# The outputs of the recurrence's chunks: the products with the state of a half of the heads ahead of those with the values, in one bank

## The chip, the core and the metric

The kernel runs on one core of a Trainium2 chip. The metric is the device time of one execution in microseconds (us). The engines of the core run side by side: TensorE (PE in the profile; PEld is its loading of weights), VectorE (DVE), ScalarE (ACT), GpSimd (POOL) and SyncE (SP), which issues the loads of the weights.

## The reference

The program is two transformer blocks in a row over a sequence of 256 tokens, 1024 features wide, the first with 16 meta tokens ahead of it (272 in all) and two layers of its own. Only the mixing of its first layer bears on the change, a linear recurrence over the tokens (16 heads of 64 features):

```python
def step(S, inp):
    r_t, w_t, k_t, v_t, a_t, b_t = inp
    sa = jnp.einsum("bhij,bhj->bhi", S, a_t)
    S = S * w_t[:, :, None, :] + sa[..., None] * b_t[:, :, None, :] + v_t[..., None] * k_t[:, :, None, :]
    y = jnp.einsum("bhij,bhj->bhi", S, r_t)
    return S, y
...
_, ys = lax.scan(step, S0, xs)
```

S is a state of 64 by 64 for each head, decayed at every token (w), with a part removed (a, b) and a key and value added (k, v). The output y of a token is the state read with its receptance r. Around this stand feed-forward blocks, norms, projections, and in the later layers attention.

## The kernel before

The weights stream in from memory in units of 512 KB. Each is split in two parts, and the matmuls of `accum` (L269, through `mm3`, L260 to L263) run three products for each tile of 128 by 128: L261, L262 and L263, which add to the same columns of a bank. These make up most of the program.

The recurrence runs over chunks (`chunks`, L923): chunk 0 is the 16 meta tokens, chunks 1 to 4 have 64 tokens each. Within a chunk, matrix products take the place of the token loop, and from chunk to chunk only the state S goes on. The heads go in pairs, two heads side by side on the 128 partitions: head h of a pair has the partitions OWN[h], 0 to 63 or 64 to 127. A step handles one half q of the heads, four pairs j, eight products (`each`, L939). The steps of a chunk c, with the lines of their matmuls:

- `keys` (L968, ck) and `values` (L982, cv): keys and values by token, on 128 partitions; GpSimd clears a part of the values' buffer UV first (L977);
- `within` (L994, cw): products of the keys with the removal keys and the receptances, masked by VectorE (L996) into a buffer G;
- `of_values` (L1020, co) and `removals` (L1028, cr): what the values and the old state add to the removals; VectorE adds them (L1030);
- `solved` (L1037, cs): the inverse of the chunk applied, copied into UV by VectorE or ScalarE;
- `state` (L1048, ct): the new state, which VectorE finishes (L1051, L1052);
- `out` (L1056, cy): the outputs, below;
- `normal` (L1067, cn): square (L1072), sum by head (matmul, L1074), logarithm and exponential on ScalarE (L1075, L1076), gain and gate on GpSimd and VectorE (L1078 to L1080). In the last two chunks the result is split for the output projection (`split`, L266, L267, into z).

An output has two parts that are added in the bank: the receptances read with the state at the chunk's start (L1063: 64 rows of the array, those of the head, and 64 columns), and the masked products G read with the values of the chunk (L1064: 128 rows, 64 columns). ScalarE or VectorE then copies the bank to the buffer yc (`evac`, L236 to L243). Chunk 0 starts from a zero state and has only the second part.

The order of these steps is a list of names written out by hand (ORDER, L57 to L65); `play` (L406) emits them in that order, and a scheduler may move single instructions past their neighbours. From chunk 1 on it reads: "... cn01 cv2 ct10 cy10 cy11 ck2 cw40 co2 cr21 cr20 cw31 cn10 cs21 cs20 ck3 cn11 ct20 ct21 cv3 cy20 co3 cw41 cr30 cr31 cv4 cy21 cs30 cs31 ct30 ct31 cn21 co4 cn20 ck4 cy30 cr40 cr41 cy31 early cs40 cy40 cn30 cn40 cs41 cy41 cn31 cn41" (the first figure is the chunk, the second the half; `early` splits the outputs of the first chunks). The output projection (`out_proj`, L372) follows; its weights are asked for ahead of time.

The buffers come from rings: `slot` (L425) has seven of one size, which take in turn the masked products G of a chunk, the inputs of the recurrence, and a room that holds the states, removals and outputs of chunk 0 (`room`, L943).

Of the kernel before, what the change touches and what calls it, by code (L numbers as in the profile page):

```python
# [30 lines left out]
OWN = (slice(0, 64), slice(64, 128))  # L31
# [71 lines left out]
class Unit:  # L103
    """Weights to stream in, the products with them, and what follows some units later; held: units before that
    this one's products still read."""
# [6 lines left out]
class Core:  # L112
# [35 lines left out]
    def call(self, fn, ahead=0):  # L148
        """fn between units; before it the parts of as many of those that follow, if they are not there yet."""
        self.items.append((fn, ahead))  # L150
# [16 lines left out]
    def hi(self, u):  # L167
        """Weights in two parts that single-pass products carry exactly: the first."""
        if not u.lo:
            return  # L170
        u.wh = self.wring.tile([128, 1024], F32R, tag="wh", name="wh", bufs=WH)[:u.p, :u.n]
        if u.hi == "A":
            self.A.activation(u.wh, u.wf[:u.p, :u.n], AF.Copy)  # L173
        else:
            self.V.tensor_copy(u.wh, u.wf[:u.p, :u.n])

    def lo(self, u):
        """And the second."""
# [5 lines left out]
    def run(self):  # L184
# [5 lines left out]
        def ahead(i, most=WH):  # L190
            """Loads, first and second parts as far ahead of unit i as their rings reach."""
# [44 lines left out]
    def evac(self, name, out, x, scale=None):  # L236
        """Copies x, by ScalarE or VectorE."""
# [17 lines left out]
    def one(self, pool, name, shape, dt=F32):  # L255
        """A tile that keeps its place as long as the pool."""
# [12 lines left out]
    def accum(self, out, wh, wl, xh, xl, kn, n, k0=0, total=None):  # L269
        """out[m] += sum over k of w[k][m] x[k], weights standing, up to n columns of x moving."""  # L270
# [6 lines left out]
    def rsqrt(self, out, x, scale, eps):  # L277
        """1 / sqrt(x * scale + eps), with a Newton step."""
# [24 lines left out]
    def rms(self, n):  # L303
        """1 / rms by token, on every partition."""
# [5 lines left out]
    def split_tile(self, k, gain, t0, n):  # L310
        """Tile k of h * gain in two parts; its squares added up."""
# [11 lines left out]

    def swiglu(self, win, wout, t0, n, hook, first=()):
        """Reads the split of h that the step before left; hook(k) follows each finished tile of h."""
# [50 lines left out]
    def out_units(self, w, kn, src, scale, t0, n, hook, k0=0, eng=lambda m: {}):  # L376
        """h += scale * x @ w, x split and by features, w given as [m][128][kn][128]; a step a tile of h."""
# [28 lines left out]
    def play(self, order, steps, units):  # L406
        """Emits the steps by name: those of units as they come, the others as calls between them."""
# [7 lines left out]

    def rwkv(self, gain, hook):
# [21 lines left out]
        # the mixed inputs of the projections  # L438
# [6 lines left out]
        def mixes(i, kind, e=None):  # L445
            """Mixed input i, a tile a call: whole, or in two parts."""
# [35 lines left out]
        def first_mix():  # L482
            """The normalised input; the mixed inputs of the keys, the decays and the removals."""
            hn, xx, last = R["hn"], R["xx"], []
            hi, lo = R["x", 2] = [self.xs.tile([128, KT, T], F32R, tag=n, name=n) for n in ("xh", "xl")]
            def mix(x, i, k):
                """Mixed input i, by VectorE, or by ScalarE and GpSimdE."""
# [69 lines left out]
        # keys  # L557
# [18 lines left out]
        def first(n, parts):  # L576
            """The first tiles of the keys and the low-rank pairs of two inputs side by side, as the inputs come."""
# [23 lines left out]
        # low-rank pairs, in float32 products  # L601
        def l1_unit(c0, parts, k0, k1, last, after=()):
            """Columns c0.. of the first factors: parts are (bank, row, width, input)."""
# [67 lines left out]
        # a, b, k by decays within a chunk  # L671
# [5 lines left out]
        def units(q):  # L677
            """1 / norm of the keys."""
# [22 lines left out]
        def over(e, j, x, s):  # L701
            """KB[place j] = x / decay, for the pairs s; the factor -1/2 of place 0 comes with the products."""
# [19 lines left out]
        # strictly lower parts of b a by chunk: diagonal blocks of 32 tokens apart from those beside them  # L722
# [43 lines left out]
        # values, receptance, bonus  # L766
# [24 lines left out]
        # gates  # L791
# [63 lines left out]
    def inverses(self, R):  # L855
        """Inverses of unit lower triangular blocks of 32 tokens (16 in the meta chunk), one per partition."""
# [66 lines left out]
    def chunks(self, R):  # L923
        """The recurrence over chunks of 64 tokens after the 16 of the meta tokens.

        Products that do not need the state of chunk c + 1 fill the waits of chunk c. The values are centred
        by head, and with them all that is linear in them, so that the normalisation needs no mean."""
# [29 lines left out]
        def keys(c):  # L957
            """Keys by token."""
# [15 lines left out]
        def values(c):  # L974
            """Values by token, centred."""
# [10 lines left out]
        def within(c, q, js=(0, 1)):  # L986
            """Products of the chunk's keys with its removal keys and receptances."""
# [11 lines left out]
        def within_meta(r):  # L999
            """The same of the meta chunk, with its removal keys (r = 0) or receptances (1)."""  # L1000
# [13 lines left out]
        def of_values(c):  # L1014
            """What the chunk's values add to the removals."""
# [40 lines left out]
        def out(c, q):  # L1056
            if "yc" not in C[c]:
                C[c]["yc"] = room(2, c)[:, :, :size(c)]
            L, p, UV, g = size(c), self.psum(), C[c]["UV"], C[c]["G"]
            for j, m, h in each(q):  # L1060
                o = p[OWN[h], j * L:(j + 1) * L]
                if c:
                    mm(o, S[c - 1][OWN[h], m], R["AR"][OWN[h], m, 1, tok(c)], start=True, stop=False)  # L1063
                mm(o, UV[:, m, h], g[:, m, h, 1], start=c == 0, stop=True)  # L1064
            self.evac("zy%d" % (2 * c + q), C[c]["yc"][:, qs[q]], p[:, :4 * L].rearrange("p (j t) -> p j t", j=4))

        def normal(c, q):  # L1067
            """Variance by head, gain, bonus and gate."""
# [35 lines left out]
    def doubles(self, R):  # L1104
        """Inverses of 64-token blocks out of those of 32."""
# [99 lines left out]
    def dsa(self, hook):  # L1205
        nc, tc, io = self.nc, self.tc, self.io
        V, A, G, mm = self.V, self.A, self.G, self.mm
        R = {}
# [837 lines left out]
```

## Time and profile before

| | us |
|---|---|
| median of 3 runs | 1602.21 |
| lowest and highest run | 1589.57 and 1602.51 |
| span of the profiled execution | 1588.7 |
| TensorE busy in it | 1527.4 |
| VectorE busy | 1020.3 |
| ScalarE busy | 732.4 |
| GpSimd busy | 334.0 |

The span goes from the first instruction to the last; a run's time is taken around it. The profiled execution's own time is not listed, so the three runs stand beside its span. In the trace each float32 product of the recurrence is two instructions of TensorE (the count behind an x). A tile form like 64*64 or 128*64 is the part of the array that an instruction uses, rows by columns. The granted clock is in parts of the full 2.4 GHz: 1.0, or 0.5 for the lower level of 1.2 GHz; between them lies a mean over a stretch with both.

### The profile page before, as it was taken

To read this page: it belongs to the slowest core of one execution; us is meant where nothing else is said; L and a number is where in the kernel's file an instruction comes from. 1 tells how busy PE (TensorE), PEld (TensorE's weight loads), DVE (VectorE), ACT (ScalarE), POOL (GpSimd) and SP (SyncE) were. 2 spreads that over 40 slices of the span, in tenths; PEclk is the share of its full clock that TensorE was granted. 3 is DMA by queue.
4 is the path that set the end of the run, shared out by engine and by line. 5 is a ranking of instruction groups with operands and counts; after the bars stand their busy time and mean duration, and the time that the engine had idled before them with its cause. 6 is when DMAs were issued, how large, how long until landed. Compare 5 with 4: busy or idle time off the path is not lost.

```text
span 1588.7 us, 30959 instructions
## 1 busy us (share of the span) xinstructions
PE 1527.4 (96%) x12612; PEld 1427.2 (90%) x12612; DVE 1020.3 (64%) x1857; ACT 732.4 (46%) x1266; POOL 334.0 (21%) x346
## 2 busy tenths in 40 slices
PE   7999989699999999999999999899999999999999
PEld 7999967568788999999999987579999978899999
DVE  6655478997444655556555569667665489886643
ACT  6544428333223544445444434655445335566532
POOL 2111034752011111001111043142110334320000
PEclk9999989798888999999999999999999999999999
DMA  7645534121101445555545552036556552265552
GB/s 224 216 173 166 178 96 141 63 92 69 41 1 41 173 173 175 171 175 191 175 174 165 172 166 77 21 112 234 186 183 180 175 167 91 85 215 186 187 195 101
DMA packets 70851, 230.63 MB, mean 145 GB/s; under 512 B 7827, under 2 KB 12468, under 8 KB 70580
## 3 DMA queue, kind: packets, MB, share of 16 engines
q1 hardware_dynamic: 68480, 225.35, 42.7%
q10 hardware_dynamic: 2228, 3.29, 0.9%
q8 instruction: 99, 1.62, 0.4%
q14 instruction: 44, 0.36, 0.1%
HBM read 226.52 MB, written 2.10 MB: 144 GB/s over the span
## 4 chain that ended last, share of the span: by engine, by line
PE 82%; DVE 12%; ACT 2%; DMA 2%; issue 1%; POOL 1%; SPq 0%; DVEq 0%; POOLq 0%; ACTq 0%
PE mm L261 22%; PE mm L262 22%; PE mm L263 22%; DVE wl L182 1%; PE mm L1064 1%; PE mm L1892 1%; PE mm L1063 1%; PE mm L1166 1%; PE mm L1165 1%; PE mm L1167 1%; DVE tf L871 1%; DMA wf<-ffn_in 1%; PE mm L994 1%; DVE u L868 1%; PE mm L1869 1%
## 5 line engine op out<-in xcount | busy, mean ns | idle before, releaser
L173 ACT ACTIVATE wh<-wf 128x1024 fp32r<-128x1024 f32 (+2 forms) x404 | 411.8, 1020 | 538.3 <-issue 284.3
L261 PE MATMUL mm<-xh,wh 128*128 128x272 f32 (+2 forms) x1888 | 544.4, 290 | 14.7 <-ACT wh L173 9.0
L182 DVE TENSOR_TENSOR wl<-wf,wh 128x1024 fp32r<-128x1024 f32 (+2 forms) x388 | 463.1, 1194 | 140.7 <-PE mm L263 96.5
L262 PE MATMUL mm<-xl,wh 128*128 128x272 f32 (+2 forms) x1888 | 542.0, 288 | 3.1 <-DVE xl L440 2.7
L263 PE MATMUL mm<-xh,wl 128*128 128x272 f32 (+2 forms) x1888 | 542.4, 288 | 1.7 <-DVE wl L182 1.7
L261 PEld LDWEIGHTS mm<-xh,wh 128*128 128x128 f32 (+1 forms) x1888 | 356.8, 190 | 21.9 <-ACT wh L173 9.9
L262 PEld LDWEIGHTS mm<-xl,wh 128*128 128x128 f32 (+1 forms) x1888 | 357.2, 189 | 7.5 <-DVE xl L440 3.8
L263 PEld LDWEIGHTS mm<-xh,wl 128*128 128x128 f32 (+1 forms) x1888 | 357.5, 190 | 3.2 <-DVE wl L182 2.7
L261 PE MATMUL mm<-hh,wh 128*128 128x272 f32 (+1 forms) x704 | 201.9, 287 | 0.0
L263 PE MATMUL mm<-hh,wl 128*128 128x272 f32 (+1 forms) x704 | 201.7, 287 | 0.0
L262 PE MATMUL mm<-hl,wh 128*128 128x272 f32 (+1 forms) x704 | 201.7, 287 | 0.0
L352 POOL TENSOR_TENSOR s<-s,rstd 128x272 f32<-128x272 f32 (+1 forms) x88 | 74.6, 849 | 442.8 <-ACT s L351 442.8
L182 POOL TENSOR_TENSOR wl<-wf,wh 128x1024 fp32r<-128x1024 f32 (+3 forms) x58 | 121.3, 2093 | 146.5 <-PE mm L263 63.5
L261 PEld LDWEIGHTS mm<-hh,wh 128*128 128x128 f32 x704 | 132.6, 188 | 0.0
L263 PEld LDWEIGHTS mm<-hh,wl 128*128 128x128 f32 x704 | 132.5, 188 | 0.0
L262 PEld LDWEIGHTS mm<-hl,wh 128*128 128x128 f32 x704 | 132.5, 188 | 0.0
L360 DVE TENSOR_TENSOR u<-mm,s 128x272 f32<-128x272 f32 (+1 forms) x88 | 38.5, 437 | 123.8 <-PE mm L263 108.2
L298 POOL TENSOR_TENSOR acc<-acc,sq 128x272 f32<-128x272 f32 (+1 forms) x48 | 41.4, 863 | 262.9 <-ACT sq L296 247.1
L350 DVE TENSOR_TENSOR t<-mm,rstd 128x272 f32<-128x272 f32 (+1 forms) x88 | 38.2, 436 | 69.8 <-PE mm L263 69.7
L261 PE MATMUL mm<-hid,wh 128*128 128x256 f32 x256 | 72.0, 281 | 0.0
L262 PE MATMUL mm<-hid,wh 128*128 128x256 f32 x256 | 72.0, 281 | 0.0
L263 PE MATMUL mm<-hid,wl 128*128 128x256 f32 x256 | 72.0, 281 | 0.0
(482 smaller groups left out, 2320.4 us busy)
## 6 DMA issues: line engine op xcount, KB each, us to landing
wf<-ffn_in SPq DMA_DIRECT2D x176, 512.0 KB, 3.6
wf<-ffn_out SPq DMA_DIRECT2D x64, 512.0 KB, 3.5
wf<-b_ff SPq DMA_DIRECT2D x64, 512.0 KB, 4.7
wf<-ffn_out SPq DMA_DIRECT2D x32, 384.0 KB, 3.1
wf<-rk_k SPq DMA_DIRECT2D x8, 512.0 KB, 3.4
wf<-rk_v SPq DMA_DIRECT2D x8, 512.0 KB, 3.8
wf<-rk_r SPq DMA_DIRECT2D x8, 512.0 KB, 3.2
wf<-rk_o SPq DMA_DIRECT2D x8, 512.0 KB, 3.2
```

The lines of the kernel that those rows point to most:

```text
L173: self.A.activation(u.wh, u.wf[:u.p, :u.n], AF.Copy)
L182: (self.V if u.lo == "V" else self.G).tensor_tensor(u.wl, u.wf[:u.p, :u.n], u.wh.bitcast(F32), op=ALU.subtract)
L261: self.mm(out, wh, xh, start=start, stop=False)
L262: self.mm(out, wh, xl, start=False, stop=False)
L263: self.mm(out, wl, xh, start=False, stop=stop)
L298: self.G.tensor_tensor(self.acc[:, :n], self.acc[:, :n], self.sq[:, :n], op=ALU.add)
L350: V.tensor_tensor(t[:, :n], st.pop(("g", m))[:, :n], r, op=ALU.mult)
L352: G.tensor_tensor(s[:, :n], s[:, :n], r, op=ALU.mult)
L360: V.tensor_tensor(u[:, :n], st.pop(("u", m))[:, :n], st.pop(("s", m))[:, :n], op=ALU.mult)
L868: e.tensor_tensor(tmp[:, x - o:y - o, :w], a[:, s, x:y, None].to_broadcast([P, y - x, w]), t[:, s:w, :w].to_broadcast([P, y - x, w]), op=A ...
L871: e.tensor_tensor(t[:, x:y, :w], t[:, x:y, :w], tmp[:, x - o:y - o, :w], op=ALU.add)
L994: mm(ps[h][:, j * w:(j + 1) * w], flat(src(c, m)[OWN[h]]), R["AR"][OWN[h], m, j0:j0 + n, tok(c)], start=True, stop=True)
```

## The change

`out` writes the eight products with the state first, then the eight with the values. Before, the two products of a head stood one behind the other. Each head's columns are still added up in the bank. The flag `start`, which marks the first product that goes to an area of a bank, was set for every product with the state; now it is set for the first one in each half of the partitions (j = 0), and the two products of a head are no longer neighbours, for which a check of the builder is turned off.

```diff
             L, p, UV, g = size(c), self.psum(), C[c]["UV"], C[c]["G"]
+            o = lambda j, h: p[OWN[h], j * L:(j + 1) * L]
+            if c:
+                for j, m, h in each(q):
+                    mm(o(j, h), S[c - 1][OWN[h], m], R["AR"][OWN[h], m, 1, tok(c)], start=j == 0, stop=False,
+                       skip_group_check=True)
             for j, m, h in each(q):
-                o = p[OWN[h], j * L:(j + 1) * L]
-                if c:
-                    mm(o, S[c - 1][OWN[h], m], R["AR"][OWN[h], m, 1, tok(c)], start=True, stop=False)
-                mm(o, UV[:, m, h], g[:, m, h, 1], start=c == 0, stop=True)
+                mm(o(j, h), UV[:, m, h], g[:, m, h, 1], start=c == 0, stop=True, skip_group_check=c > 0)
```

The lines behind it move down by four: L1063 becomes L1065, L1064 becomes L1068, L1074 becomes L1078, L1079 becomes L1083. The rest of the diff takes out comments.

TensorE's order in chunk 2, from the new state and the values of the next chunk (L1048, L982) to the first step of the outputs, before; mm is a bank, AR holds the receptances, room the state, UV the values:

```order
L1048 MATMUL mm_4998<-UV_4808,KBt_3913 64x64
L1048 MATMUL mm_5009<-UV_4808,KBt_3913 64x64 x8
L982 MATMUL mm_5022<-mats_81,vf_3054 64x128 x4
L1048 MATMUL mm_4998<-UV_4808,KBt_3913 64x64 x7
L982 MATMUL mm_5028<-mats_81,vf_3054 64x128 x4
L1063 MATMUL mm_5034<-AR_2503,room_4593 64x64
L1064 MATMUL mm_5034<-G_4715,UV_4808 64x64
```

And now:

```order
L1048 MATMUL mm_4998<-UV_4808,KBt_3913 64x64
L1048 MATMUL mm_5009<-UV_4808,KBt_3913 64x64 x8
L982 MATMUL mm_5022<-mats_81,vf_3054 64x128 x4
L1048 MATMUL mm_4998<-UV_4808,KBt_3913 64x64 x7
L982 MATMUL mm_5028<-mats_81,vf_3054 64x128 x4
L1065 MATMUL mm_5034<-AR_2503,room_4593 64x64 x8
L1068 MATMUL mm_5034<-G_4715,UV_4808 64x64 x8
L1020 MATMUL mm_5052<-UV_5020,G_4638 64x64 x16
```

Before, the last two rows are followed by seven more such pairs; now the eight products with the state are one row, and the eight with the values another, with L1020 (co3) right behind them as before.

TensorE's order behind the second step of chunk 1 (mm_4851), before; G_4715 are the masked products of chunk 2:

```order
L1063 MATMUL mm_4851<-AR_2503,room_3954 64x64
L1064 MATMUL mm_4851<-G_4336,UV_4352 64x64
L968 MATMUL mm_4869<-mats_81,kbx_2510 128x128 x4
L968 MATMUL mm_4875<-mats_81,kbx_2510 128x128 x4
L994 MATMUL mm_4882<-AR_2503,kbx_2510 128x128 x4
L994 MATMUL mm_4883<-AR_2503,kbx_2510 128x128 x4
L1020 MATMUL mm_4894<-UV_4808,G_4715 64x64
L1028 MATMUL mm_4912<-room_4593,AR_2503 64x64 x8
L1028 MATMUL mm_4922<-room_4593,AR_2503 64x64 x3
L1020 MATMUL mm_4894<-UV_4808,G_4715 64x64 x15
L1028 MATMUL mm_4922<-room_4593,AR_2503 64x64 x5
```

And now:

```order
L1065 MATMUL mm_4851<-AR_2503,room_3954 64x64 x8
L1068 MATMUL mm_4851<-G_4336,UV_4352 64x64 x8
L968 MATMUL mm_4869<-mats_81,kbx_2510 128x128 x4
L968 MATMUL mm_4875<-mats_81,kbx_2510 128x128 x4
L994 MATMUL mm_4882<-AR_2503,kbx_2510 128x128 x4
L994 MATMUL mm_4883<-AR_2503,kbx_2510 128x128 x4
L1020 MATMUL mm_4894<-UV_4808,G_4715 64x64
L1028 MATMUL mm_4912<-room_4593,AR_2503 64x64 x7
L1020 MATMUL mm_4894<-UV_4808,G_4715 64x64 x15
L1028 MATMUL mm_4912<-room_4593,AR_2503 64x64
L1028 MATMUL mm_4922<-room_4593,AR_2503 64x64 x8
```

The keys (L968) and masked products (L994) stand behind the step as they did; the removals of the first half (L1028) go around L1020 a little differently, four products of them behind it that stood ahead.

## Rows read from the trace of the kernel before

**Rows 1.** The page: its first line, and TensorE in its first part
```profile
span 1588.7 us, 30959 instructions
...
PE 1527.4 (96%) x12612; PEld 1427.2 (90%) x12612; DVE 1020.3 (64%) x1857; ACT 732.4 (46%) x1266; POOL 334.0 (21%) x346
```

**Rows 2.** Stretches: us, busy of PE, PEld, DVE, ACT, POOL (instructions), clock, DMA share, GB/s
```profile
425.83:437.04 11.21, 11.21 (x67) 8.01 (x65) 1.19 (x4) 1.06 (x3) 0.68 (x1) 0.63 0.01 1
437.04:445.85 8.81, 8.81 (x81) 7.90 (x82) 3.90 (x7) 1.57 (x4) 1.63 (x2) 0.50 0.00 0
...
453.40:457.51 4.11, 4.11 (x39) 3.10 (x40) 1.35 (x4) 0.59 (x1) 0.00 (x0) 1.00 0.00 0
...
462.50:466.75 4.25, 4.25 (x33) 3.13 (x32) 0.00 (x0) 0.00 (x0) 0.00 (x0) 0.95 0.00 0
...
473.54:477.65 4.11, 4.11 (x33) 3.03 (x33) 1.02 (x3) 1.64 (x4) 1.40 (x1) 1.00 0.02 4
...
478.63:482.69 4.06, 4.06 (x38) 2.98 (x35) 1.21 (x3) 0.39 (x2) 0.95 (x1) 1.00 0.00 0
484.04:487.90 3.86, 3.86 (x31) 2.84 (x30) 0.85 (x2) 0.89 (x2) 0.00 (x0) 1.00 0.00 0
...
490.03:497.55 7.52, 7.48 (x40) 4.93 (x36) 2.60 (x7) 1.68 (x6) 0.41 (x1) 0.51 0.01 2
497.55:503.90 6.35, 5.47 (x22) 5.29 (x23) 2.04 (x5) 2.41 (x6) 0.00 (x0) 0.50 0.00 0
```

**Rows 3.** The chain that ended last, 400 to 505 us: start, us, what
```profile
421.93 0.60 PE mm L1064 x16
...
429.44 0.40 PE mm L1064 x2
...
443.90 1.90 PE mm L1020 x30
...
453.47 0.25 PE mm L1063 x2
453.72 0.26 PE mm L1064 x2
...
457.58 0.93 PE mm L1020 x31
...
459.60 1.08 PE mm L1028 x32
...
477.72 1.08 PE mm L1028 x32
...
482.76 0.61 PE mm L1037 x16
```

**Rows 4.** The timeline of the output projection: start, us, engine, line, operation
```profile
502.18 0.43 PE L261 MATMUL mm<-z,wh 128*128 128x272 f32 x1
...
502.40 0.43 PE L262 MATMUL mm<-z,wh 128*128 128x272 f32 x1
...
502.63 0.43 PE L263 MATMUL mm<-z,wl 128*128 128x272 f32 x1
```

**Rows 5.** The timeline of VectorE behind the second step of chunk 1
```profile
436.74 2.48 DVE L996 TENSOR_TENSOR G<-mm,tri 128x512 f32<-128x512 f32 x4 [9.91 <-PE mm L1063]
```

**Rows 6.** The timeline behind the second step of chunk 2
```profile
466.75 1.97 PE L1037 MATMUL mm<-room,Tt 64*64 64x64 f32 x32
466.86 0.59 ACT L239 ACTIVATE UV<-mm 64x512 f32<-64x512 f32 x1 [7.72 <-PE mm L1064]
...
468.20 0.36 ACT L239 ACTIVATE UV<-mm 64x256 f32<-64x256 f32 x1
...
468.66 0.59 PE L1048 MATMUL mm<-UV,KBt 128*64 128x64 f32 x6
```

**Rows 7.** The timeline behind the last step
```profile
498.43 1.22 PE L1074 MATMUL mm<-sqc,mats 128*128 128x256 f32 x2 [0.92 <-ACT sqc L1072]
...
502.02 0.43 DVE L267 TENSOR_TENSOR z<-bb,z 128x256 fp32r<-128x256 f32 x1 [0.48 <-ACT z L266]
```

## The prediction

> **What bounds the kernel now.** I read the page's first part, then the stretches of the recurrence, then the chain of waits inside them. TensorE is busy for 96% of a span of 1588.7 us [rows 1], so a saving on it counts wherever it has no idle time. The changed step is called eight times with the state, twice (for the two halves of the heads) in each of chunks 1 to 4, all between 425.8 and 497.6 us. In its stretches TensorE is busy for the whole length, while VectorE and ScalarE are busy for 1.2 of the first 11.2 us and for nothing at all of 462.50 to 466.75 [rows 2]. So here TensorE alone sets the pace, and it does so with tiny matmuls: a step is 8 products with the state and 8 with the values, and each of them is two instructions in the trace.
>
> What one costs stands in the chain: a product with the state holds it for 0.25 us, the next with the values for 0.26, at full clock [rows 3], at 453.47 and 453.72; 16 make the 4.11 us of 453.40 to 457.51 [rows 2]. At the lower clock one holds it for 0.40, at 429.44 [rows 3]. The same shapes cost a quarter of that where they stand with their own kind. L1028 is the twin of the state half (weights and outputs 64 by 64, the halves of the array in turn): 32 instructions in 1.08 us, 0.034 each, at 459.60 [rows 3]. L1020 is the twin of the values half (128 rows, 64 columns, 64 moving): 31 in 0.93, 0.030 each. The values half of the meta chunk, which has no state, stands alone already: 16 instructions in 0.60, though with 16 columns moving [rows 3]. So of 0.257 us per product some 0.19 is neither streaming nor loading; it comes with the change from a product of one kind to one of the other.
>
> Two explanations fit that far. One is the change of the part of the array in use, from 64 rows to 128 and back, at which the array empties. The other is that the second product adds to the columns that the first has just written. The rows are against the second: L261, L262 and L263 add to the same columns one right after the other, and start 0.22 us apart at the lower clock [rows 4], which is 272 columns at 1.2 GHz (0.227) and leaves nothing for a wait.
>
> The Trainium skill has the first as a rule (TensorEngine Tiling (Array Packing), Key Properties): changing the tiling mode, not just the tile, drains TensorE. The trace agrees, by the 0.257 us beside 0.034 and 0.030.
>
> **The change part by part.** It removes and adds no instruction: 16 products a step before and after, the same operands, one evacuation. It turns 16 changes of kind a step into 2. On VectorE and ScalarE one instruction each changes places with its neighbour, on TensorE besides four products of L1028 are on the other side of L1020, and on GpSimd and SP the order is what it was, so only TensorE's own time and what it uncovers count.
>
> The new price of a step: the state half like L1037 x16 directly behind a product with the values, 0.61 us at 482.76 [rows 3], which has one change in it; the values half like 16 of L1020, 0.48, with one change, about 0.6. I take 1.2. From below it is 32 instructions at 0.03, 1.0; from above each change keeps its full 0.19 on top of the streaming, 1.4. Between them lie only 1.5 us over eight steps.
>
> Step by step, at the profiled execution's own times [rows 2]:
> - Steps of chunk 1: 11.21 us become 2.4. Gain 8.8. The granted clock averages 0.63 there: it is 1.0 for about 2.9 us and then 0.5, which is 1.2 GHz. The price of 1.2 a step assumes that it doesn't fall.
> - The stretch behind it, 437.04 to 445.85, is all at 0.5. It came back at the end of a dense block of L1020 (30 in 1.90 us, twice the price at full clock [rows 3]). The fall came inside a row of products that mostly wait; the dense blocks of small products ahead of that row had left the clock at 1.0. I take it that dense halves keep it up: 8.81 becomes 4.4. Gain 4.4; if it falls all the same, nothing here, and 2 less in the line above.
> - What is late next there: VectorE waits 9.9 us for a matmul of L1063 [rows 5], because the products of chunk 2 (G, L996) go into the buffer that holds the first state, whose last reader is the second step of chunk 1. That wait ends with the state half, so L996's 2.5 us move forward with the rest and end near the time at which L1020 wants them. I book nothing.
> - Chunk 2: 4.11 and 4.25 become 2.4. Gain 6.0. Behind the second step stands ScalarE's queue, which that step keeps from starting: from L1037's start at 466.75 four ScalarE items end at 468.56, and only then L1048 goes [rows 6]. L1037 itself took that long, as the clock was low. At full clock it would take 1.1 and TensorE would wait for the rest, so the 1.9 us stay; no gain and no loss.
> - Chunk 3: 4.11 and 4.06 become 2.4. Gain 5.8.
> - Chunk 4, first half: 3.86 and one product that stands ahead of a variance product (0.25) become 1.2. Here the cover goes: ScalarE's logarithm and exponential for the step before ran under the products and now stand ahead of the evacuation. I book 0.4 for it. Gain 2.5.
> - Chunk 4, second half, with a variance product in it: 490.03 to 497.55, 7.52, mostly at 0.5. It becomes 0.6 for the state half, 0.6 for the variance product (half of the 1.22 that one takes at the lower clock [rows 7]) and 0.6 for the values half, 1.8. Gain 5.7.
> - The tail: from the evacuation to the last part of z is VectorE's and ScalarE's, and the output projection's second half needs it [rows 7]. Half of L1074's 1.22 would come back at full clock; I book 0.5.
>
> Sum: 8.8 + 4.4 + 6.0 + 5.8 + 2.5 + 5.7 + 0.5 = 33.7 us, 2.1% of the span. Behind it the feed-forward blocks are TensorE's alone, with weights loaded ahead while the DMA engines lie idle here, so the gain goes through to the end. The span would be 1588.7 - 33.7 = 1555.0. What lies around it isn't shown: the three runs are 1589.57, 1602.21 and 1602.51, so it is 0.9 us if the profiled execution was like the lowest, 13.5 if it was like the median. From the median I get 1602.2 - 33.7 = 1568.5, and forecast 1569. That these runs differ by 13 us with the same program is the widest single term of my range.
>
> **Rivals.**
> 1. The halves gain, but the clock falls as before, by its own timing. Then the stretch behind chunk 1 gives nothing (-4.4), chunk 1's steps 2 less, the last block about 2 less: gain 25, 1577. For it: the clock also fell near 466 and 490 with TensorE busy throughout. Against it: each fall lies in or behind a row of alternating products.
> 2. Only the state half gets cheaper. Its neighbours use different halves of the rows, those of the values half all use 128, so a load of weights might not run beside a product there. Then the 8 products with the values keep 0.257 each, a step costs 2.06 + 0.61 = 2.7, and the gain is 1.4 in each of five steps, about 6 in chunk 1 and 2 at the end: 15, 1587. Against it: L1020's 0.030 an instruction [rows 3].
> The Trainium skill states what would do this (TensorE: Matmul & The Clock Gate, Part 3, What overlaps and what doesn't): weight loads overlap running matmuls only when the row groups differ. The trace disagrees for this shape, by the 0.93 us for 31 of L1020.
> 3. Slower: uncovered waits on VectorE and ScalarE leave TensorE with holes from chunk 1 on, and the clock goes to 0.5 and stays there. From 437.04 to 497.55 some 33 us are not these steps (60.5 less 4.11, 4.25, 4.11, 4.06, 3.86 and 7.52); 12 of them are at 0.5 already (8.8, and about 3 behind 466.75, where L1037 runs at half speed [rows 6]), so 21 more are added; the steps at twice 1.2 still give back about 20. It is then even, and each microsecond of work of the projection and the blocks behind that stays at 0.5 adds one: after 16 us of them it is 1% slower, with the whole projection and the first tiles behind it (26) 1628. For it: the gain in cover is real, and after the last fall half speed lasted to 503.9 [rows 2]. Against it: it needs the clock to stay low through dense work, and dense work brought it back each time.
> 4. No change by over 1%: the recurrence's own chain (removals, inverse, state, through VectorE and ScalarE) sets the pace, so that what TensorE gives up turns into waits. From L1028 at 459.60 to the next at 477.72 is 18.1 us [rows 3]; with both steps cut it is 12.2, while the chain in it is about 2 for the removals and 7 from L1037 at 466.75 to the next step at 473.54 [rows 2, 6]. It would have to grow by 3 us in each chunk to eat a third of the gain; to get below 16 us of gain takes more. I give it little.
>
> **How the numbers follow.** The drain goes and the clock holds, 0.56: 1569. Rival 1, 0.25: 1577. Rival 2, 0.09: 1587. Rival 4, 0.07: 1590. Rival 3, 0.03. A measurement of this kernel tells about 1% from no change, 16 us: faster is below 1586.2, slower above 1618.2. The first two cases and a third of rival 2 are faster, 0.84; with some of rival 4 I say 0.86; same 0.11, slower 0.03. The range goes from the gain in full with a median like the lowest run of before (1589.6 - 33.7 = 1556) to rival 2 (1587).
>
> **What would show it right or wrong.** Right: in the chain of the changed kernel each step appears as a piece of 16 for the state (L1065) and one of 16 for the values (L1068), 0.5 to 0.65 us each, and no piece of two at 0.25; VectorE's 9.9 us behind the state half shrinks; the granted clock is 1.0 from chunk 1 to the next chunk. Rival 1 shows as 0.5 in that stretch. Rival 2 shows as pieces of L1068 of 2 us. Rival 4 shows as idle time of TensorE with VectorE or ScalarE as its releaser. The forecast is wrong if L1068's instructions still stand 0.1 us apart or more, or if new idle time on TensorE between 425 and 500 us is over 10 us.

## The result, and the profile after

| | before | after |
|---|---|---|
| median of 4 runs each, us | 1595.89 | 1553.22 |
| lowest and highest run | 1588.59 and 1602.51 | 1552.98 and 1554.51 |
| span of the profiled execution | 1588.7 | 1551.4 |
| its own time | not listed | 1553.19 |
| mean granted clock in it | 0.971 | 0.984 |

The first of these medians stands beside the 1602.21 of three runs from which the forecast started; one run has been added. The changed kernel takes 0.973 of the time of before, interval 0.970 to 0.977. The forecast was 1569 us with a range of 1556 to 1587: the direction is right, and the time is 2.8 us below the range. The two medians lie 42.7 us apart and the two spans 37.3; the difference is that the profiled execution of before was at the low end of its kernel's runs.

The page of the changed kernel, its first line and TensorE in its first part, against [rows 1]:

```profile
span 1551.4 us, 30960 instructions
...
PE 1489.5 (96%) x12612; PEld 1398.2 (90%) x12612; DVE 1018.1 (66%) x1857; ACT 731.8 (47%) x1266; POOL 334.7 (22%) x346
```

The instructions of the engines are the same in number. The span is 37.3 us shorter, TensorE's busy time 37.9, and the other engines' is where it was within 2.2: what went was TensorE's own time.

The stretches of the changed kernel that answer to [rows 2]: the two steps of chunk 1, the stretch from there to chunk 2, the two steps of chunk 2, the two of chunk 3, the first 9.5 us of the output projection, and the recurrence as a whole (columns as in [rows 2]):

```profile
425.06:427.51 2.45, 2.45 (x65) 2.18 (x66) 1.46 (x4) 0.98 (x3) 0.27 (x1) 1.00 0.03 7
427.51:439.97 12.46, 12.46 (x199) 10.88 (x200) 9.66 (x21) 4.74 (x10) 1.98 (x3) 1.00 0.01 1
439.97:441.20 1.23, 1.23 (x39) 1.16 (x40) 1.20 (x4) 0.59 (x1) 0.00 (x0) 1.00 0.00 0
446.19:447.44 1.25, 1.25 (x35) 1.11 (x36) 0.00 (x0) 0.00 (x0) 0.00 (x0) 1.00 0.00 0
453.58:454.81 1.23, 1.23 (x35) 1.10 (x36) 0.69 (x3) 1.23 (x4) 0.00 (x0) 1.00 0.00 0
455.89:456.97 1.08, 1.08 (x34) 0.95 (x32) 0.95 (x2) 0.41 (x2) 1.08 (x2) 1.00 0.00 0
...
465.51:475.00 9.49, 9.49 (x77) 9.49 (x77) 4.60 (x8) 4.33 (x8) 0.00 (x0) 1.00 0.01 4
...
425.00:500.00 75.00, 72.10 (x1001) 66.72 (x1001) 50.70 (x95) 38.95 (x79) 13.40 (x16) 1.00 0.20 68
```

A step takes 1.08 to 1.25 us in place of 3.9 to 5.6 (7.5 with a variance product in it), and the column of the clock is 1.00 in every row, where five of the rows of the same work before had 0.50 to 0.95. TensorE idles for 2.9 of the 75 us.

The chain that ended last in the changed kernel, against [rows 3] (start, us, what): the steps of chunk 1; the second step of chunk 2 and what follows it; the first half of chunk 4 behind its products with the state.

```profile
425.06 0.61 PE mm L1065 x16
425.67 0.62 PE mm L1068 x16
426.29 0.61 PE mm L1065 x16
426.90 0.62 PE mm L1068 x16
...
446.80 0.64 PE mm L1068 x16
...
447.46 0.59 ACT UV L239
...
448.81 0.37 ACT UV L239
...
...
458.04 0.64 PE mm L1078 x2
...
458.71 0.48 ACT sqc L1079
...
459.21 0.42 ACT sqc L1080
459.63 0.28 ACT room L239
```

Pieces of two at 0.25 us have become pieces of sixteen at 0.61. Behind chunk 2's second step the chain now goes through four ScalarE items, from 447.44 to 449.22, where L1037 at half clock covered them before [rows 6]. TensorE itself works for most of that time; its timeline there, with its idle time in brackets:

```profile
447.35 1.15 PE L1037 MATMUL mm<-room,Tt 64*64 64x64 f32 x32
448.67 0.33 PE L1048 MATMUL mm<-UV,KBt 128*64 128x64 f32 x2 [0.17 <-DVE UV L243]
449.22 0.57 PE L1048 MATMUL mm<-UV,KBt 128*64 128x64 f32 x12 [0.23 <-ACT UV L239]
```

So it idles for 0.40 us there. In chunk 4 ScalarE's logarithm and exponential (L1079, L1080) stand ahead of the copy of the outputs.

VectorE's wait for the first state's last reader, against [rows 5] (who waits for whom: us in total, times, longest):

```profile
DVE G L996 <- PE mm L1065: 1.0, 1, 1.0
```

It was 9.9 us.

Put side by side by TensorE's own sequence (its pieces are the same products in nearly the same order), the changed kernel is 0.8 us ahead at the first of the steps, 34.2 us at the projection's first piece (465.51 in place of 499.66), 36.1 some 20 us into the projection, and 37.3 at the end. So the recurrence and the projection's start give 35.3; the remaining 2.0 are no work of the change: 0.8 lie ahead of it, 1.2 behind it, where the largest piece, 1.8, is a short fall of the clock near 1360 us that of these two executions only the one of before has. The profiles of experiments 7 and 9 have a fall at the same place of the program, so it needs no products in turn.

### The profile page after: what moved, and what is told of

It is laid out like the page before. It is cut to its first block, busy times and chain, and to the rows that moved or that the text cites. A ratio compares the mean times of both kernels' runs of the same rounds, so it can differ in the third digit from the quotient of the medians.

```text
span 1551.4 us, 30960 instructions
## 1 busy us (share of the span) xinstructions
PE 1489.5 (96%) x12612; PEld 1398.2 (90%) x12612; DVE 1018.1 (66%) x1857; ACT 731.8 (47%) x1266; POOL 334.7 (22%) x346
## 4 chain that ended last, share of the span: by engine, by line
PE 82%; DVE 12%; ACT 2%; DMA 1%; issue 1%; POOL 1%; SPq 0%; DVEq 0%; POOLq 0%; ACTq 0%
PE mm L261 23%; PE mm L262 23%; PE mm L263 23%; DVE wl L182 1%; PE mm L1896 1%; PE mm L1170 1%; PE mm L1169 1%; PE mm L1171 1%; DMA wf<-ffn_in 1%; DVE tf L871 1%; PE mm L1873 1%; PE mm L994 1%; PE mm L1898 1%; PE mm L1840 1%; PE mm L982 1%
```

## The experiments

The theory at this point: a change of the number of rows in use (64 and 128) costs some 0.15 to 0.2 us, the drained rows of products pull the granted clock down, both are gone, the sum of the prediction holds, and the base from which it was taken off does not. Five of the experiments test the mechanism and its places (2 to 6), three whether more is to be had (7, 9, 10), and four the base and the spread (1, 8, 11, 12). In the diffs below `o(j, h)` are the columns of a head in the bank.

**1. The kernel before again, unchanged.** What lies around the span, and what spreads?

> The kernel before, unchanged, to see what its two levels of time are (two runs near 1589, two near 1602). Theory A (the alternating products let the clock fall, and how much of the recurrence lies at 1.2 GHz differs from run to run): the runs near 1602 have a span about 12 us longer and a lower mean granted clock, by about 0.008, than those near 1589, whose clock is 0.971. Theory B (the 12 us lie around the span, in the launch): all runs have a span near 1589 and a clock of 0.971.

Measured: 1596.18 us (1588.94 to 1602.48, 12 runs) beside 1594.08 of 17 runs of the same kernel, ratio 1.0006 (0.9987 to 1.0025). The time is 1.74 to 1.93 us above the span in every run, whether it is long or short. The spans go from 1587.1 at a mean clock of 0.974 to 1600.6 at 0.965, with runs at all values between, so it is a spread and not two levels. In the mean clock that is 0.009 of 1594 us, which at 0.5 in place of 1.0 are 29 us, half of them lost where TensorE sets the pace: 14, and the spans differ by 13.5. The mean clock doesn't explain all of it: the spans at 0.965 alone go from 1594.8 to 1600.6. So the profiled execution of before was a run of some 1590.5 us, and the median from which the forecast started lies at the upper end, where the runs of this group have a mean clock of 0.965 or 0.966.

**2. In turn as before, but in two banks**, so that no product adds to what its neighbour has just written. The products with the state are left out of the output; a copy of one of their columns by VectorE stands for their use.

```diff
+            p2 = self.psum() if c else None
             for j, m, h in each(q):
                 if c:
-                    mm(o, S[c - 1][OWN[h], m], R["AR"][OWN[h], m, 1, tok(c)], start=True, stop=False)
-                mm(o, UV[:, m, h], g[:, m, h, 1], start=c == 0, stop=True)
+                    mm(p2[OWN[h], j * L:(j + 1) * L], S[c - 1][OWN[h], m], R["AR"][OWN[h], m, 1, tok(c)], start=True, stop=True)
+                mm(o(j, h), UV[:, m, h], g[:, m, h, 1], start=True, stop=True)
```

> The two kinds of products stand in turn as before, but into two banks, so that none adds to columns just written; the state's part is left out of the outputs, and VectorE reads a column of its bank. Theory A (the change between 64 and 128 rows of the array empties it): a product in turn still holds TensorE for 0.25 to 0.26 us at full clock, 4.1 us a step where the order is in turn. Rival B (adding to columns that the product before has just written waits for it): 0.03 us an instruction, about 1.1 us a step.

Measured: 1582.56 us, one run, span 1580.8. The scheduler happened to pull the products of chunk 1's steps apart into pieces of sixteen and ten, so its time tells little; its pieces tell more. The chain of this kernel, in the first step of chunk 1 and in the next chunk, where the products still stand in turn:

```profile
427.44 0.61 PE mm L1064 x16
428.05 0.61 PE mm L1065 x16
...
443.64 0.26 PE mm L1064 x2
443.90 0.26 PE mm L1065 x2
444.16 0.25 PE mm L1064 x2
```

In turn they take 0.25 and 0.26 as before, in two banks as in one, and grouped 0.61. Adding in the same bank is not the price.

**3. In turn and in one bank as before, but the product with the state on all 128 rows**, like the one with the values. It then adds the other head's rows too, so the outputs are other numbers.

```diff
-                    mm(o, S[c - 1][OWN[h], m], R["AR"][OWN[h], m, 1, tok(c)], start=True, stop=False)
+                    mm(o(j, h), S[c - 1][:, m], R["AR"][:, m, 1, tok(c)], start=True, stop=False)
```

> The two kinds in turn as before and in one bank, but the product with the state takes all 128 rows (both heads of the pair, so the outputs are not the reference's): the same part of the array as the product with the values. Theory A (emptying at a change between 64 and 128 rows): no change is left, 0.03 to 0.06 us a product, 1.0 to 1.2 us a step, and a total near 1553. Rival B (adding to columns just written): 0.25 us a product, 4.1 us a step, total near 1589.

Measured: 1553.51 us, one run, span 1551.7, clock 0.984, the time of the changed kernel. The timeline of TensorE in chunk 1's steps:

```profile
425.89 0.34 PE L1063 MATMUL mm<-AR,room 128*64 128x64 f32 x4
426.01 0.34 PE L1064 MATMUL mm<-G,UV 128*64 128x64 f32 x4
426.13 0.34 PE L1063 MATMUL mm<-AR,room 128*64 128x64 f32 x4
```

The two kinds still alternate, four instructions every 0.12 us, and nothing waits: 0.03 an instruction. Two kinds of operands, two destinations and two lines cost nothing; with 64 rows against 128 the same alternation cost 0.257 a product. So it is the change of the rows, shown by this run beside the second one. It is the rule of the Trainium skill that changing the tiling mode drains TensorE (TensorEngine Tiling (Array Packing), Key Properties), and the trace agrees, with 0.03 against 0.13 an instruction. That the products with the values, all on 128 rows, stand 0.03 apart with their weight loads is against one sentence of the Trainium skill's other page (TensorE: Matmul & The Clock Gate, Part 3, What overlaps and what doesn't), by which loads run beside products only where the row groups differ. The paragraph ahead of that sentence, though, names loads into a background weight buffer as a second case; which of the two holds here no run shows.

**4. Half as many changes as before**: both heads of a pair with the state, then both with the values; 8 changes a step, where before had 16 and the changed kernel has 2.

```diff
+            for j, m in four(q):
+                if c:
+                    for h in range(2):
+                        mm(o(j, h), S[c - 1][OWN[h], m], R["AR"][OWN[h], m, 1, tok(c)], start=True, stop=False, skip_group_check=True)
+                for h in range(2):
+                    mm(o(j, h), UV[:, m, h], g[:, m, h, 1], start=c == 0, stop=True, skip_group_check=c > 0)
```

> Two products with the state, then the two with the values, pair by pair: 8 changes of kind a step, between 16 (before) and 2 (after). If the cost is per change: 4.11 and 1.22 us a step give 0.206 us a change, so 2.45 us a step at full clock. If it is per neighbour in the same columns (Rival B): each product with the values has one other product in between, so something between 1.2 and 2. The clock: if a row of mostly waiting products brings it down, less of the recurrence is at 0.5 than before; total 1563 to 1575.

Measured: 1561.81 us (1559.58 to 1564.3, 4 runs), ratio 0.979 (0.976 to 0.981), 1.2 us below the range expected. The stretch of the recurrence (columns as in [rows 2]), with the clock at 1.00:

```profile
425.00:475.00 50.00, 47.64 (x778) 38.94 (x773) 27.08 (x63) 22.09 (x52) 9.96 (x12) 1.00 0.01 4
```

The chain in chunk 2's first step:

```profile
444.98 0.26 PE mm L1064 x4
445.24 0.27 PE mm L1067 x4
445.51 0.26 PE mm L1064 x4
```

A block of four instructions (two heads) takes 0.26, which is what a block of two took in turn; the step takes 2.11 us (444.98 to 447.09), less than the 2.45 expected. Through blocks of 4 (0.265) and of 16 (0.615) goes a line of 0.029 an instruction and 0.147 a change; the block of 2 lies 0.05 above it. So the price of a change was mis-sized in the prediction: 0.15 between blocks of more than one product, not 0.19. Why a second head in a block adds nothing is not shown: the products of a pair with the state use different halves of the rows, but those with the values both use all rows and cost the same. Over the recurrence this kernel gains 28.7 us, 6.6 less than the changed one; eight steps of 2.11 in place of about 1.22 make 7.1.

**5. and 6. The change in chunk 1 only, and in chunks 2 to 4 only.** Each is the changed kernel with a condition on the chunk, `grouped = c == 1` in the one and `grouped = c != 1` in the other; where it is false the products stand in turn:

```diff
+            grouped = c == 1
+            if c and grouped:
+                for j, m, h in each(q):
+                    mm(o(j, h), S[c - 1][OWN[h], m], R["AR"][OWN[h], m, 1, tok(c)], start=j == 0, stop=False, skip_group_check=True)
             for j, m, h in each(q):
+                if c and not grouped:
+                    mm(o(j, h), S[c - 1][OWN[h], m], R["AR"][OWN[h], m, 1, tok(c)], start=True, stop=False)
```

> Grouped in chunk 1 alone, in turn in chunks 2 to 4. Theory A (each change of kind costs its time, and rows of products in turn let the clock fall): the two steps of chunk 1 take 1.22 us each, the clock stays at 1.0 up to chunk 2, and the gain up to the end of chunk 1's successors is 13 to 16 us; six steps stay at 4.1 or more, so the median is 1575 to 1583, and the runs still spread over 5 us or more, by what the clock does in chunks 2 to 4. Rival C (the clock falls by its own timing, whatever the order of the products): the clock falls in or behind chunk 1 all the same, and the gain there is 7 to 9.

> Grouped in chunks 2 to 4, in turn in chunk 1. Theory A: the clock falls in chunk 1's steps or behind them as before and costs up to 6 us there; six steps at 1.22 us give 18 us, and with the clock at 1.0 at the end 20 to 24: median 1568 to 1576, a spread of a few us. Rival C: falls to 0.5 in chunks 3 and 4 as before, median 1574 to 1582.

Measured: 1578.8 us (1575.42 to 1586.41, 4 runs), ratio 0.990 (0.987 to 0.993), with chunk 1 alone; 1566.79 (1565.08 to 1571.17, 4 runs), ratio 0.983 (0.980 to 0.987), with chunks 2 to 4. The stretches of the recurrence with chunk 1 alone grouped:

```profile
425.00:450.00 25.00, 25.00 (x408) 21.58 (x405) 14.58 (x32) 7.94 (x17) 2.26 (x3) 1.00 0.01 2
450.00:475.00 25.00, 24.59 (x284) 18.68 (x283) 8.24 (x19) 8.17 (x19) 4.62 (x5) 0.96 0.00 1
475.00:505.00 30.00, 28.18 (x193) 25.40 (x194) 15.73 (x28) 14.78 (x30) 4.02 (x6) 0.81 0.21 70
```

And with chunks 2 to 4 grouped:

```profile
425.00:450.00 25.00, 25.00 (x230) 20.22 (x230) 9.14 (x19) 5.61 (x12) 2.31 (x3) 0.66 0.00 1
450.00:475.00 25.00, 23.49 (x489) 20.14 (x488) 15.20 (x35) 12.17 (x29) 6.50 (x7) 1.00 0.01 3
475.00:505.00 30.00, 28.61 (x235) 28.42 (x232) 20.99 (x33) 17.62 (x33) 4.64 (x6) 1.00 0.40 130
```

Where the products are grouped the clock stays at 1.00; where they stand in turn it falls, in these rows of products or behind them (0.96 and 0.81 in the later stretches of the one kernel, 0.66 in the first of the other). By TensorE's sequence the first gives 13.6 us and the second 22.5, together 36.1 beside 35.3 for both at once: the parts add up, and the fall is of their own making, not the program's timing.

**7. The products with the state earlier.** As a step of their own (`out_state`, named cx in the order), ahead of the products with the values: directly behind the removals or solved values, which use 64 rows as well, so that one more change goes and TensorE has work while it waits.

```diff
-          "cs11 cn00 gate7 cw20 cy01 ct11 cn01 cv2 ct10 cy10 cy11 ck2 cw40 co2 cr21 cr20 cw31 cn10 cs21 cs20 "
+          "cs11 cx10 cx11 cn00 gate7 cw20 cy01 ct11 cn01 cv2 ct10 cy10 cy11 ck2 cw40 co2 cr21 cr20 cw31 cn10 "
+          "cs21 cs20 cx20 cx21 ck3 cn11 ct20 ct21 cv3 cy20 co3 cw41 cr30 cr31 cv4 cy21 cs30 cs31 cx30 cx31 ct30 "
+          "ct31 cn21 co4 cn20 ck4 cy30 cr40 cr41 cx40 cx41 cy31 early cs40 cy40 cn30 cn40 cs41 cy41 cn31 cn41 ").split()
...
+        def out_state(c, q):
+            L, p = size(c), self.psum()
+            C[c]["yp", q] = p
+            for j, m, h in each(q):
+                mm(p[OWN[h], j * L:(j + 1) * L], S[c - 1][OWN[h], m], R["AR"][OWN[h], m, 1, tok(c)], start=j == 0, stop=False,
+                   skip_group_check=True)
```

> The state half of the outputs is a step of its own, behind the inverse's products (L1037), or in chunk 4 behind the removals (L1028), which use the same 64 by 64 part of the array; the values half stays where it is, mostly beside products on 128 rows. Theory A: the two changes of a step are nearly gone, 0.15 us each, 2 to 2.5 us in all, and the state halves fill TensorE's wait for ScalarE behind L1037 in chunk 2 (another 0.8): median 1549 to 1552. Rival D (what is saved on TensorE turns into waits on VectorE's and ScalarE's chain): 1553, no change against the changed kernel.

Measured: 1552.76 us (1551.84 to 1554.75, 4 runs), ratio 0.974 (0.971 to 0.976); the changed kernel beside it (below) 1553.97. Theory A's range is missed by 0.8, and the 1.2 us to the changed kernel are less than either kernel's runs differ by. By TensorE's sequence it is 2.8 us ahead of the changed kernel's first profile up to chunk 4, 1.8 at the projection's first piece, and 0.9 at the end. The chain in chunk 4:

```profile
454.05 1.51 DVE z L267
455.56 0.34 DVE room L1030
...
456.04 0.68 PE mm L1037 x16
```

VectorE's subtraction of the early split stands ahead of its addition of the removals, and L1037 waits for that; TensorE idles for 0.98 us. So the earlier products are a gain of 2.8 us, of which chunk 4 takes 1.0 back. Most of the rest of the lead goes in a fall of the clock between 1305 and 1325 us (0.91 there, 1.00 in the changed kernel), which is not the change's.

**8. The changed kernel again**, beside it.

> The changed kernel once more beside the others, for its spread and as the reference of e7: median 1553, a span 1.8 us below each run's time, all runs within 3 us, a clock of 0.984 in each.

Measured: 1553.97 us (1553.5 to 1557.05, 4 runs), ratio 0.975 (0.972 to 0.977); the runs lie 3.6 us apart, a little more than expected.

**9. The seventh kernel with both halves of that subtraction on GpSimd; 10. the same with another order at the end of chunk 4; 11. the changed kernel a third time.**

```diff
-                self.split(z[:, 0, qs[q], :e], z[:, 1, qs[q], :e], R["bb"][q][:, :, :e], (V, G)[q])
+                self.split(z[:, 0, qs[q], :e], z[:, 1, qs[q], :e], R["bb"][q][:, :, :e], G)
...
-          "ct31 cn21 co4 cn20 ck4 cy30 cr40 cr41 cx40 cx41 cy31 early cs40 cy40 cn30 cn40 cs41 cy41 cn31 cn41 ").split()
+          "ct31 cn21 co4 cn20 ck4 cy30 cr40 cr41 cx40 cx41 cy31 cs40 cs41 early cy40 cn30 cy41 cn40 cn31 cn41 ").split()
```

> The kernel e7_placed (the state halves as steps of their own, right behind the removals and the solved values), with both halves of the subtraction in the early split of z on GpSimd instead of one on VectorE. In e7_placed VectorE's subtraction (1.51 us, behind ScalarE's first part) stood ahead of its addition of the removals, L1030, and chunk 4's L1037 went only at 456.0. Theory: that subtraction is the whole of what chunk 4 lost; without it L1037 of chunk 4 goes 2 us or more earlier and the lead of e7_placed behind chunk 3, some 2 to 3 us over the changed kernel, stays to the end: median 1549 to 1551.5, and 1.5 to 3 us below the changed kernel beside it. Rival: ScalarE's own queue of chunk 4 (squares, logarithms, exponentials, copies) ends last there, and takes it back: 1552 to 1554, within 1 us of the changed kernel. Second rival: the split's second half comes later from GpSimd (its work is slower), and the projection waits for it: above 1554.

> The same as e9_gpsimd_split, with the end of the order written by hand changed too: the solved values of both halves of chunk 4 first, then the early split, then the outputs and their normalisation. Theory: ScalarE's parts of the early split no longer stand ahead of the copies that the solved values and outputs need, so 1 us or so more than e9_gpsimd_split: 1548 to 1551. Rival: the split then ends late and the first products of the projection wait for z, so nothing or a loss against e9_gpsimd_split: 1552 to 1555.

> The changed kernel once more, beside the two others on the same chip: 1552.5 to 1555.5, all runs within 4 us of each other, as before, with the time 1.7 to 2.0 us above the span in each run. If the narrow spread of the changed kernel had been chance, a run at 1560 or above would show.

Measured, six runs each: 1552.64 us (1552.2 to 1557.34), 1554.53 (1553.34 to 1557.8) and 1557.76 (1553.55 to 1560.19); ratios 0.973, 0.974 and 0.976, each within 0.004. The chain of the ninth kernel in chunk 4 has no VectorE or GpSimd ahead of L1037:

```profile
455.02 0.62 PE mm L1069 x16
455.63 0.61 PE mm L1037 x16
```

But the first of them goes at 455.63, 0.4 us earlier, or 1.0 with the later start of this execution's recurrence (0.6) taken off, and not 2 or more: TensorE's own products now fill the time up to there, and the 0.98 us that it had idled was all there was to get. With it the loss of chunk 4 is gone, as the theory had it; the size was wrong. It stays 2.9 us ahead of the changed kernel's profiled execution from the recurrence on, until a fall of the clock between 1315 and 1335 us (0.91 there, 1.00 in the changed kernel) takes 1.9 of it; in time it is 0.6 to 5.1 us below the three groups of the changed kernel, and these differ by 4.5 among themselves. So its median is the lowest of all, by an amount that these runs don't tell from nothing. The tenth has 1.3 less of a lead behind the recurrence than the ninth: its rival holds.

The third group of the changed kernel had a run at 1560.19, and its median is 2.3 us above the range expected, so the narrow spread of its first two groups was in part chance. Its profiled execution is 4.5 us behind the first one already at 315 us, and 4.3 at the end. TensorE between 20 and 40 us, in this execution:

```profile
20.00:40.00 20.00, 16.89 (x130) 16.37 (x129) 10.23 (x22) 11.61 (x16) 3.30 (x3) 1.00 0.63 165
```

In the changed kernel's first profile:

```profile
20.00:40.00 20.00, 19.80 (x156) 19.50 (x155) 13.45 (x26) 11.97 (x17) 3.36 (x3) 1.00 0.67 170
```

TensorE is busy for 2.9 us less there at the same clock of 1.00, while the first weights come in and the DMA engines are busy 0.63 to 0.67 of the time: a second source of spread, 3.7 us by 40 us, that is not the clock. (A fall of the clock behind it, 0.92 between 40 and 60 us, adds 0.9.)

**12. The kernel before a third time**, for a profile of a longer run.

> The kernel before once more, profiled, to see where a longer run of it spends its time. The two profiled executions so far lay at the low end (spans 1588.7 and 1587.8, mean clocks 0.971 and 0.974), while the spans of its runs go up to 1601 at 0.965. Theory: whatever this run's span is over 1588, the excess stands as further time at half clock in the rows of alternating products and right behind them (425 to 505 us), since the kernels in which these rows are gone spread less. Rival: the excess stands elsewhere, in the start (loads that come late, before 40 us) or in the feed-forward and attention blocks, and has nothing to do with the change. If the run is another low one (span below 1590, 0.973 or 0.974), it tells nothing between the two.

Measured: 1592.12 us, span 1590.3, clock 0.972, so once more near the low end. Its stretches at the start and in the recurrence:

```profile
20.00:40.00 20.00, 17.68 (x131) 17.17 (x130) 10.99 (x23) 12.26 (x17) 3.30 (x3) 0.95 0.67 175
...
425.00:450.00 25.00, 25.00 (x283) 20.74 (x284) 10.99 (x25) 7.36 (x16) 3.29 (x5) 0.86 0.01 1
450.00:475.00 25.00, 24.62 (x299) 20.25 (x295) 10.01 (x23) 6.70 (x15) 2.27 (x3) 0.86 0.01 2
475.00:505.00 30.00, 28.16 (x211) 21.48 (x210) 7.84 (x20) 8.95 (x23) 3.88 (x4) 0.72 0.00 1
```

It starts 4 us late as the eleventh does, and in the recurrence the same program has its half clock at other places than the first profile (there 0.66, 0.93 and 0.77 in these three stretches), for about the same sum. Where a run of 1600 us spends its time was not seen in any profile. What speaks for these rows of products is only the spread: 14.4 us over all 53 runs of before, 11.0 over four with chunks 2 to 4 in turn, 6.1 over four with chunk 1 in turn, 7.2 over the 14 runs of the changed kernel.

## Why the prediction was wrong in its time and right in its mechanism

The sum, term by term. What came is read from the chain: how much earlier the same work starts behind a step than ahead of it.

| term | predicted | came | from |
|---|---|---|---|
| chunk 1's steps | 8.8 | 8.8 | 11.21 to 2.45 |
| the stretch behind, at full clock | 4.4 | 3.9 | 16.36 to 12.46 |
| chunk 2 | 6.0 | 5.9 | 4.11 and 4.25 to 1.23 and 1.25 |
| chunk 3 | 5.8 | 5.9 | 4.11 and 4.06 to 1.23 and 1.08 |
| between these steps | 0 | 0.6 | from 466.75 on, 6.79 to 6.14 |
| chunk 4, first half, to ScalarE's copy | 2.5 | 2.7 | 5.31 to 2.66 |
| second half, the same | 5.7 | 5.1 | 9.55 to 4.41 |
| the tail and the projection's start | 0.5 | 2.5 | half clock to 503.9 is gone |
| sum, of the terms before rounding | 33.7 | 35.3 | |

ScalarE's copies of the outputs of chunk 4's two halves and the projection's first piece, in the chain of before:

```profile
488.00 0.39 ACT room L239
...
497.55 0.39 ACT room L239
...
499.66 0.23 PE mm L261
```

And of the changed kernel, where the first copy stands at 459.63 (above):

```profile
464.04 0.28 ACT room L239
...
465.51 0.13 PE mm L261
```

**The step that failed is the base**, where the prediction put "From the median I get 1602.2 - 33.7 = 1568.5". The 33.7 had been worked out on an execution with a span of 1588.7, and what lies around a span was taken as 13.5 us. It is 1.74 to 1.94 us in all 93 runs for which both are known. So the profiled execution was one of some 1590.5 us, and the two numbers of one subtraction came from different executions. From 1590.5 the sum gives 1556.8, inside the range and 3.6 above the 1553.2 of the changed kernel's profiled execution. Of the forecast's miss of 15.8 us, 11.7 are the base (1602.2 in place of 1590.5), 1.6 the sum, 2.0 what the two executions differ by outside the change, and 0.5 the rounding up.

Behind it lies that the spread was taken as a constant around the work. Experiment 1 shows the larger part of it as granted clock inside the span: the longer runs have a lower mean clock. That a change that takes half clock away takes more from such a run than from the profiled one fits the medians (42.7 us apart where the spans are 37.3), but in no profile of a long run was it seen. The prediction had the low end of its range as lowest run less the sum, 1556, with no margin for a sum that is 1.6 us small and for 2.0 us that have nothing to do with the change, and so missed it.

**The terms.** The price of a step was right (1.08 to 1.25 for 1.2), since it was taken from rows with one change each; the price of a change on its own was mis-sized, 0.15 in place of 0.19 (experiment 4), which weighs little at two changes a step. Two slips of the prediction weigh nothing: over eight steps its bounds of 1.0 and 1.4 a step lie 3.2 us apart and not 1.5; and its 0.257 us is for a product of two instructions, beside 0.034 and 0.030 for one, so like for like it is 0.13. The tail was mis-sized: 0.5 for the variance product's clock, while the fall in the second half of chunk 4 reached into the projection, whose products stood 0.23 apart at half clock and stand 0.13 apart now; that is 1.9 of the 2.5. The rows had it: 497.55 to 503.90 at 0.50 [rows 2]. The stretch behind chunk 1 gave 0.5 less, and ScalarE's queue, which was to cost 0.4 in the first half of chunk 4, cost 0.3 there, and 0.6 in the second half, where nothing was booked (459.29 to 459.63, and 463.42 to 464.04).

**The mechanism** stands. That the change of rows is the price and adding in the bank is not was argued from [rows 4]; experiments 2 and 3 show it. That the halves hold the clock at 1.0 was a guess with a chance of 0.56; experiments 4 to 6 bear it out.

**The rivals.** The first, the clock falls by its own timing: refuted by 1.00 from 425 to 500 us and by experiment 5, in which only the chunks left in turn have a fall; experiment 6 shows the same. The second, half of the cheapening: L1068 takes 0.61 for 16, not 2.06. The third, holes that hold the clock down: TensorE idles 2.9 of 75 us and the clock stays. The fourth, the recurrence's own chain: waits on ScalarE and VectorE did appear, but TensorE idles only 0.4 us behind chunk 2's second step, half of the 0.8 that the prediction's 1.9 less 1.1 leaves, and 1.1 and 1.4 in chunk 4, where 0.9 each stood before. Experiments 7 and 9 gain 2.8 and 2.9 us up to the projection; in the ninth only 0.7 of that is idle time filled, since TensorE idles for 2.2 of the same 75 us.

## What to carry to other kernels

Small matmuls that change between 64 and 128 rows pay for each change what five or six of their instructions cost. Group them by rows, or give both the same rows; products that add to one bank needn't stand next to each other.

Such a row counts as busy in the profile while it does little, and the granted clock may fall in it or behind it: read the clock by stretches, and add what the half clock costs in the work behind the row, to its last microsecond.

Subtract a gain from the execution on which it was worked out. Where runs spread by as much as the gain, find first what a run's time is beside its span and whether mean clock explains the spread.

## What the runs showed of the hardware that was not expected

- A block of two products in turn costs as much as a block of one: 0.26 us for four instructions as for two, between changes of the rows. From 4 to 16 instructions it grows by 0.029 each.
- The places of the fallen clock differ from run to run of one program (0.66, 0.93, 0.77 in three stretches of the recurrence in one profile, 0.86, 0.86, 0.72 in another), while their cost is nearly the same.
- With 8 changes a step the clock did not fall in the recurrence, with 16 it did, though TensorE counts as busy throughout in both.
